# Two more seven-product units in the last down projection of an fp32 encoder layer, parked sums added a part earlier, parked data reloaded at other times

## The chip, the cores and the metric

The program runs on one core of a Trainium2 chip. The metric is the device time of one execution in microseconds (us); a time of three runs is their median.

## What is computed

One hybrid encoder layer on 256 tokens of width 2048, all in float32: a mixing sub-layer (neighbourhood attention beside a recurrent block), a SwiGLU feed-forward sub-layer, and a gated per-layer embedding, each with root-mean-square norms before and after. The change lies in the feed-forward sub-layer, cut from the reference to its core:

```python
fn = rms_norm(h, g_ffn_pre[i])                                              # (256, 2048)
ff = (jax.nn.silu(fn @ w_ffn_gate[i]) * (fn @ w_ffn_up[i])) @ w_ffn_down[i] # 2048 -> 5632 -> 2048
h = h + rms_norm(ff, g_ffn_post[i])
gate = jax.nn.sigmoid(rms_norm(h, g_ple_pre[i]) @ w_ple_gate[i])
h = h + rms_norm(gate * (p[i] @ w_ple_proj[i]), g_ple_post[i])
```

## The kernel before

**Matmuls.** Every float32 operand is split into a high part (rounded to the matmul's own float32 form) and a low part (the rest). A product of a 128x128 activation block and a 128x512 weight block is three matmuls on TensorE (PE): high times high, low times high, high times low. Weights come from HBM in tiles of two 128-row blocks by 512 columns (512 KB). SyncE (SP) issues the load into a raw buffer (`wr`, `third`, or a parked corner named `lower`, `lower2` or `ple`); ScalarE (ACT) casts it to `wh` (L624); VectorE (DVE) subtracts to get `wl` (L637); then the matmuls of that tile run. There are four `wh`/`wl` buffer pairs and, for part of the program, a fifth, `w`, which stands in the buffer that later holds the gain vector. A tile's raw buffer is free for the next load when DVE has subtracted it.

**Parts.** The 5632 hidden features are worked through in 11 groups of 512 columns (`f` = 0 to 10), in three parts: `PARTS = ((0, 4), (4, 8), (8, 11))`. In a part, each `f` has a gate and an up product with 2048 input features; ACT applies silu, DVE multiplies (`mid`, L1731) and transposes it in 32x32 blocks (L335), and 16 small DMAs (`mT<-mid`, L345) finish the transposition; ACT and DVE split the result to `mid0h/l`, `mid1h/l`, `mid2h/l`. Then the part's share of the down projection runs: four chunks of 512 output columns, taken in two pairs, `c` = 0 and 2. The third part has 12 feature blocks of 128, so each pair goes over six steps `k` = 0, 2, ..., 10.

**Parked sums.** The down products of parts 0 and 1 are copied out of PSUM by ACT (L1802) and written by SP (L1805) to two HBM tensors, `parts[0]` and `parts[1]`. In part 2 they return: `reload_sums` loads `parts[0]` into `mg` by SP (L1827) and adds `parts[1]` to it with accumulating DMAs issued by GpSimd (POOL, L593). The last chunks are then added to `mg` (L1472) and multiplied by the gain `g_ffn_post` (L1484). The residual stream `h` and a half of the embedding product `ple` are parked in HBM too, and their buffers lent out (`lower` stands in `h0`, `sums` in `h1`, `lower2` in `mg0`, `s` in `mg1`); `reload_h`, `reload_half` and `next_gain` bring back what is needed.

**Seven products.** A pair of chunks, the two row halves of the 256 tokens and the two blocks of a step `k` make eight block products. Some steps are done with seven (a 2x2 scheme in Strassen's manner), with sums of activations (`S1` to `S7`, made by DVE in `sums_of` and `mid_sums`) and sums of weights (DVE in `sum_stream`, one term by an accumulating DMA of POOL in `last_sum`). Such a unit runs as `four` (four products, two tiles), then, after DVE and ACT have put the four results together in the accumulators (`made_of_four`: ACT L730 and L724, DVE L732 to L739), `two` (two products) and a share of `one`. The `four`s are placed inside the group before, by `FOURS`; `TAKEN` says after which steps the `two`s and the `one`s come. Gate and up use it for `f` = 2 to 10, the down pairs for `k` in `DOWN_KS = {0: (0, 2), 2: (0, 2, 4)}`, in parts 0 and 1 only:

```python
SEVEN_PARTS = PARTS[:2]
...
mid, ks, DOWN_KS[c] if PARTS[part] in SEVEN_PARTS else (), apart=2 if end else 0,
```

**Order.** The PE's order is that of the segments. The other engines' order is made when the program is built: a planner (`Plan`) gives each operation an engine, a cost and a time from which it may start, and emits the one that can start first. On the chip each engine and each queue keeps that order, so an instruction that waits holds back all behind it on its engine.

Of the kernel before, what the change touches and what calls it, by code (L numbers as in the profile page):

```python
# [39 lines left out]
RING = 5  # L40
DOWN_KS = {0: (0, 2), 2: (0, 2, 4)}
SEVEN_F = range(2, 11)
SEVEN_PARTS = PARTS[:2]

SWAPPED = [
    (lambda f: (("w_ffn_gate", f), ("w_ffn_up", f)), SEVEN_F, SEVEN_KS),
    *(
        (lambda c: (("w_ffn_down", c), ("w_ffn_down", c + 1)), (c,), [4 * f0 + k for k in ks])
        for f0, _ in SEVEN_PARTS for c, ks in DOWN_KS.items()
    ),  # L50
]

# [183 lines left out]
def layer(ctx: ExitStack, tc: tile.TileContext, a: dict, out: bass.AP):  # L236
# [130 lines left out]
    def done(event):  # L367
        event.t = plan.now
# [63 lines left out]
    class Group:  # L432
# [39 lines left out]
        own, twos = None, None  # L472

        def issue(self, nxt):
            if self.own is None:
                self.own = []
            self.twos = []
            if nxt:
                nxt.own = []
            n, m = len(self.rest), len(self.rest) - self.apart  # L480
            begin = not self.sevens
# [12 lines left out]
            for i, k in enumerate(self.rest[:m]):  # L494
                for j, at in enumerate(FOURS[n, len(nxt.sevens)] if nxt and nxt.sevens else ()):
                    if i == at:
                        nxt.four(j)
                for ch, w, n0 in self.chunks:
                    seg(ch, w, n0, self.lhs, [k], begin and i == 0, i == n - 1,
                        self.after if i == m // 2 else None)  # L500
                take()
            for ch, w, n0 in self.chunks if self.apart else ():
                seg(ch, w, n0, self.lhs, self.rest[m:], first=False)

    TAKEN = {(3, 5): (0, 2, 3), (2, 6): (0, 1, 1, 1)}
    FOURS = {(8, 3): (3, 5, 7), (5, 3): (2, 3, 4), (6, 3): (3, 4, 5), (5, 2): (2, 4), (6, 2): (3, 5)}
    fours = {}

# [118 lines left out]
    def lo_stream():  # L627
        last_one = max(f[1] for f in fours.values())
        for i in range(len(tiles)):
            at_lo[0] = i  # L630
            for j in pieces(i):
                n = j.stop - j.start
                yield ev_hi[i, j.stop]
                src = raws[i] if n == 2 else raws[i][:, j, :]
                m = slice(j.start, j.start + src.shape[1])
                yield dve(src.shape[1] * N, give=gives.get(i) or raw_kind(i) if j.stop == 2 else None)
                nc.vector.tensor_tensor(  # L637
                    out=los[i][:, m, :], in0=src, in1=f32(his[i][:, m, :]), op=ALU.subtract
                )
                done(ev_lo[i, j.stop])  # L640
            raws.pop(i)
            if i == half_end:
                plan.add(reload_half(), plan.now + 76.0)
            if i in fours:
                plan.add(last_sum(i), plan.now, -2 * SOON)
            if i == last_one:
                done(ev_ple)

    MM = 0.216
    MM4 = 0.86  # L650
# [92 lines left out]
    def two_products(group, j, i):  # L743
        (C1, _, _), (C2, _, _) = group.chunks
        kx = group.sevens[j][1]
        s = group.lhs.sums[kx]
        plan.main(0, ev_lo[i, 2], group.lhs.ev[kx + 1], group.made)
        product(C1.accs[0], block(group.lhs, kx + 1, 0), i, 0, seeded=True)
        product(C2.accs[0], s["S4"], i, 1, seeded=True)
        spent(i)  # L750
        if i == last_two:
            for t in range(NT):
                plan.add(reload_sums(0, t), plan.clk["pe"] + 9.0 + 4.0 * t)
                plan.add(reload_sums(1, t), plan.clk["pe"] + 28.0 + 5.0 * t)
# [634 lines left out]
    t2 = {}  # L1389

    class Halves:
        def __init__(self, pool, n):
            self.tiles = [
                pool.tile([P, D], F32, tag=f"{n}{t}", name=f"{n}{t}") for t in range(NT)
            ]

# [204 lines left out]
            nc.sync.dma_start(spill[t], t2["h"].tiles[t])  # L1601
        done(ev_spilled)

    halves_back = []

    def reload_h(t):
        if "back" not in t2:
            t2["back"] = Halves(t2["pool"], "h")
        yield dma(1024)
        nc.sync.dma_start(t2["back"].tiles[t], spill[t])  # L1610
        halves_back.append(t)
        if len(halves_back) == NT:
            t2["h"] = t2["back"]
            done(ev_back)
# [128 lines left out]
    def carried(mid, kk0, mT):  # L1743
        summed = any(kk0 <= kx < kk0 + 4 for kx in mid.ev_sums)
        for b in range(0, 4, 2):
            kk = kk0 + b
            i, j = divmod(kk, 8)
            hi, lo = mid.tiles(i)
            yield from split(
                *(by_tile(x[:, j : j + 2, :]) for x in (hi, lo)), mT[:, b : b + 2], 2 * S,  # L1750
                give="mt" if b and not summed else None,
            )
            mid.pair(kk)
        if summed:
            plan.add(mid_sums(mid, kk0, mT), plan.now)

    def mid_sums(mid, kk0, mT):

# [35 lines left out]

    def down_post(part, c):
        def post(ch):
            e = None
            for t in range(NT):
                yield act(N, take=None if t else "mid")
                if not t:  # L1800
                    e = mid_tile()
                nc.scalar.copy(e[:, t, :], ch.accs[t])  # L1802
            ch.release()
            yield dma(512)
# [8 lines left out]
    ev_parts = []  # L1813

    def reload_sums(part, t):
        assert len(ev_parts) == 8
        if "mg_back" not in t2:
            t2["mg_back"] = t2["mg"] = Halves(t2["pool"], "mg")
        if part:
            there = Event()  # L1820
            yield from added(t2["mg"].tiles[t], parts[part][t], there)
            yield there
            if t == NT - 1:
                done(ev_sums_back)
        else:
            yield dma(1024)
            nc.sync.dma_start(t2["mg"].tiles[t], parts[0][t])  # L1827

    def after_ffn():
        return next_norm(ffn, hP, rstd_p, ev_rp, ("ple", "g_ple_post"))  # L1830
# [20 lines left out]
    for part, (f0, f1) in enumerate(PARTS):  # L1851
# [11 lines left out]
        for c in range(0, 4, 2):  # L1863
            slot = ring()
            end = last_part and c
            groups.append(Group(
                [
                    (Chunk(
                        sub_post(ffn, c + i, True, after_ffn) if last_part
                        else down_post(part, c + i), slot=slot,  # L1870
                    ), "w_ffn_down", (c + i) * N)
                    for i in range(2)
                ],
                mid, ks, DOWN_KS[c] if PARTS[part] in SEVEN_PARTS else (), apart=2 if end else 0,
                after=load_sqrt if end else None,
            ))
    n_ffn = len(segs)
# [176 lines left out]
    for i in range(min(fours), max(f[1] for f in fours.values())):  # L2054
        if i % (W_BUFS + MORE_W) < MORE_W:
            more_w[i] = i % (W_BUFS + MORE_W)
    for n, i in enumerate(sorted(lower)):
# [5 lines left out]
        gives[last] = tuple(f"t{j}" for j in js)  # L2063
    twos = [(j, i) for f, g, j, i in (s for s in segs if s[0] is two_products)]
    last_two = max(i for _, i in twos)
    half_end = max(f[1] for f in fours.values())
    i0 = segs[-1][-1]
    keep.update(range(i0, i0 + 8))
# [120 lines left out]
```

## Time and profile before

| | before |
|---|---|
| time of three runs, us | 1163.18 (1162.78 to 1164.9) |
| profiled execution, us | 1162.47 |
| its span from first to last instruction, us | 1160.7 |
| mean granted TensorE clock | 0.997 |
| PE busy, us | 1146.8 |
| DVE busy, us | 887.0 |
| ACT busy, us | 710.5 |
| POOL busy, us | 124.7 |

The span is cut by stage. Part 0's down products run from 509.5 us, part 1's from 759.1 us and part 2's from 982.1 us to about 1053 us; after them come the norm, the transposition of `h` and the gated embedding. Matmuls overlap, so their durations add up to more than the time between their starts: a stall is read from the starts.

### The profile page before, as it was taken

What the parts mean: (1) busy time and instruction counts of PE and PEld (TensorE: products, weight loads), DVE (VectorE), ACT (ScalarE), POOL (GpSimd) and SP (SyncE); (2) the same over time, 40 slices, a digit from 0 to 9 for tenths busy, and PEclk for the clock granted to TensorE, in tenths of its full rate; (3) what the DMA queues carried; (4) which work ended last, traced back from release to release, by engine and by line L of the source; (5) the groups of instructions that cost most, each with busy time, mean ns of one, the idle gap of its engine ahead of it and who ended that gap; (6) DMA issues with size and microseconds to landing.
All of it is one profiled execution on the core that took longest, in us unless ns stands there. A gap on an engine that the chain in (4) does not pass through costs nothing.

```text
span 1160.7 us, 15071 instructions
## 1 busy us (share of the span) xinstructions
PE 1146.8 (99%) x5219; PEld 951.5 (82%) x5219; DVE 887.0 (76%) x1107; ACT 710.5 (61%) x946; POOL 124.7 (11%) x202
## 2 busy tenths in 40 slices
PE   9999999999999999999999999999999999999997
PEld 8888888888888878888888888888888888777786
DVE  6678787888468878988778898988777985368565
ACT  6777777875556545655556566565565654256664
POOL 0000000000000023031000213312000321200000
PEclk9999999999999999999999999999999999999999
DMA  8867566545686987877876786778787677985771
GB/s 307 301 185 232 175 181 207 176 151 198 218 294 191 308 238 250 249 216 215 283 238 229 244 246 203 233 239 248 218 296 236 199 224 245 268 286 195 216 249 73
DMA packets 112732, 265.86 MB, mean 229 GB/s; under 512 B 39184, under 2 KB 46096, under 8 KB 110992
## 3 DMA queue, kind: packets, MB, share of 16 engines
q1 hardware_dynamic: 101744, 247.76, 63.2%
q0 software_dynamic: 10480, 16.79, 8.6%
q8 instruction: 41, 0.67, 0.2%
q10 hardware_dynamic: 432, 0.35, 0.1%
q14 instruction: 35, 0.29, 0.1%
HBM read 247.03 MB, written 9.44 MB: 221 GB/s over the span
## 4 chain that ended last, share of the span: by engine, by line
PE 88%; DMA 5%; DVE 3%; ACT 2%; issue 1%; POOL 1%; SPq 0%; ACTq 0%; DVEq 0%; POOLq 0%
PE acc L673 23%; PE acc L672 23%; PE acc L671 23%; PE acc L684 5%; PE acc L682 5%; PE acc L683 5%; DMA mT<-mid 2%; DMA wr<-in_w_ffn_down 1%; DMA wr<-in_w_ple_gate 1%; DVE wl L637 1%; ACT wh L624 1%; PE tr L326 1%; POOL mT L345 1%; PE warm L2098 0%; PE pg L357 0%
## 5 line engine op out<-in xcount | busy, mean ns | idle before, releaser
L637 DVE TENSOR_TENSOR wl<-wr,wh 128x1024 fp32r<-128x1024 f32 (+1 forms) x313 | 374.7, 1210 | 142.0 <-ACT wh L624 137.5
L624 ACT CAST wh<-wr 128x1024 fp32r<-128x1024 f32 (+1 forms) x313 | 324.7, 1043 | 213.0 <-PE acc L672 134.8
L672 PE MATMUL acc<-wh,hT_mix_lo 128*128 128x512 f32 x400 | 155.9, 390 | 0.3 <-DVE hT_mix_lo L315 0.3
L671 PE MATMUL acc<-wh,hT_mix_hi 128*128 128x512 f32 x400 | 156.0, 390 | 0.0
L673 PE MATMUL acc<-wl,hT_mix_hi 128*128 128x512 f32 x400 | 155.7, 389 | 0.0
L345 POOL DMA_DIRECT2D mT<-mid x152 | 89.0, 596 | 563.1 <-ACT wh L624 401.7
L673 PE MATMUL acc<-wl,hT_hi 128*128 128x512 f32 x320 | 124.6, 390 | 0.0
L671 PE MATMUL acc<-wh,hT_hi 128*128 128x512 f32 x316 | 124.5, 394 | 0.0
L672 PE MATMUL acc<-wh,hT_lo 128*128 128x512 f32 x316 | 123.2, 390 | 0.0
L624 ACT CAST wh<-ple 128x1024 fp32r<-128x1024 f32 (+1 forms) x54 | 53.4, 989 | 68.0 <-DVE ple L576 34.4
L672 PEld LDWEIGHTS acc<-wh,hT_mix_lo 128*128 128x128 f32 x400 | 75.1, 188 | 16.4 <-DVE hT_mix_lo L315 1.0
L671 PEld LDWEIGHTS acc<-wh,hT_mix_hi 128*128 128x128 f32 x400 | 75.1, 188 | 15.5
L673 PEld LDWEIGHTS acc<-wl,hT_mix_hi 128*128 128x128 f32 x400 | 75.1, 188 | 15.5
L637 DVE TENSOR_TENSOR wl<-ple,wh 128x1024 fp32r<-128x1024 f32 (+1 forms) x54 | 61.5, 1142 | 12.7 <-ACT wh L624 12.2
L673 PEld LDWEIGHTS acc<-wl,hT_hi 128*128 128x128 f32 x320 | 60.3, 188 | 12.9
L672 PEld LDWEIGHTS acc<-wh,hT_lo 128*128 128x128 f32 x316 | 59.4, 188 | 11.5
L671 PEld LDWEIGHTS acc<-wh,hT_hi 128*128 128x128 f32 x316 | 59.5, 188 | 11.4
L593 POOL DMA_DIRECT2D ple<-in_w_ffn_up x27 | 24.0, 891 | 234.7 <-DVE wl L637 195.9
L671 PE MATMUL acc<-wh,hT_ffn_hi 128*128 128x512 f32 x104 | 40.9, 393 | 0.8 <-ACT hT_ffn_hi L313 0.8
L672 PE MATMUL acc<-wh,hT_ffn_lo 128*128 128x512 f32 x104 | 40.8, 393 | 0.5 <-DVE hT_ffn_lo L315 0.5
L673 PE MATMUL acc<-wl,hT_ffn_hi 128*128 128x512 f32 x104 | 40.5, 390 | 0.0
L671 PE MATMUL acc<-wh,mid2h 128*128 128x512 f32 x96 | 38.3, 399 | 2.2 <-ACT wh L624 2.2
(431 smaller groups left out, 2422.6 us busy)
## 6 DMA issues: line engine op xcount, KB each, us to landing
wr<-in_w_ffn_gate SPq DMA_DIRECT2D x78, 512.0 KB, 5.4
wr<-in_w_in SPq DMA_DIRECT2D x77, 512.0 KB, 4.6
wr<-in_w_ffn_down SPq DMA_DIRECT2D x65, 512.0 KB, 5.5
wr<-in_w_ffn_up SPq DMA_DIRECT2D x49, 512.0 KB, 5.1
wr<-in_w_out SPq DMA_DIRECT2D x32, 512.0 KB, 4.4
wr<-in_w_ple_gate SPq DMA_DIRECT2D x32, 512.0 KB, 4.6
lower<-in_w_ffn_up SPq DMA_DIRECT2D x22, 512.0 KB, 6.0
ple<-in_w_ffn_up POOLq DMA_DIRECT2D x27, 256.0 KB, 4.3
```

What stands on the lines that cost most here:

```text
L326: nc.tensor.transpose(tr[:, b, t * P : (t + 1) * P], e[:, t, sl], ident)
L345: (nc.gpsimd if i in pool else nc.sync).dma_start(dst[32 * j : 32 * j + 32, :, :, i, :], src[32 * i : 32 * i + 32, :, :, j, :],)
L593: nc.gpsimd.dma_start(dst, src, accum_op=ALU.add)
L624: nc.scalar.copy(his[i][:, 0 : src.shape[1], :] if n == 2 else his[i][:, j, :], src)
L637: nc.vector.tensor_tensor(out=los[i][:, m, :], in0=src, in1=f32(his[i][:, m, :]), op=ALU.subtract)
L671: nc.tensor.matmul(accs[t], hi[:, sl], his[i][:, j, :], start=st, stop=False, **group)
L672: nc.tensor.matmul(accs[t], lo[:, sl], his[i][:, j, :], start=False, stop=False, **group)
L673: nc.tensor.matmul(accs[t], hi[:, sl], los[i][:, j, :], start=False, stop=sp, **group)
L682: nc.tensor.matmul(dst, x[0], wh, start=start, stop=False, skip_group_check=seeded)
L683: nc.tensor.matmul(dst, x[1], wh, start=False, stop=False, skip_group_check=seeded)
L684: nc.tensor.matmul(dst, x[0], wl, start=False, stop=stop, skip_group_check=seeded)
```

## The change

- **Seven products in the last part.** Pair `c` = 0 of part 2 does steps `k` = 0 and 2 as units of seven products (the weights' host layout follows). Its `four`s stand in the gate and up group of `f` = 10. The sums of its activations are made 20 us later on the planner's clock than the split they come from.
- **The last features used later.** The first step of the next pair (`c` = 2, `k` = 0) is put inside pair `c` = 0, after its step `k` = 6 (`pair`, `ahead`), so that steps 8 and 10, which use the last group's features, stand behind it.
- **Parked sums added early.** Part 1's down chunks are no longer copied by ACT. POOL loads the slice of `parts[0]`, DVE adds the accumulators to it, and POOL writes the sum to `parts[1]`. The accumulating DMAs of `reload_sums` are gone. Part 0's slices are written by POOL instead of SP.
- **Parked data back at other times.** `mg` is loaded once, from `parts[1]`, after the last `one` of gate and up; `h0` and `h1` after the last `two`; the gain right after the last use of `w`; the half of `ple` 46 instead of 76 on the planner's clock after the last `four`.

The diff, cut to what the prediction speaks of:

```diff
-        for f0, _ in SEVEN_PARTS for c, ks in DOWN_KS.items()
+        for f0, _ in PARTS for c, ks in DOWN_KS.items() if not c or f0 != PARTS[-1][0]
...
+        def pair(self, i):
+            n = len(self.rest)
+            for ch, w, n0 in self.chunks:
+                seg(ch, w, n0, self.lhs, [self.rest[i]], not self.sevens and i == 0, i == n - 1,
+                    self.after if i == (n - self.apart) // 2 else None)
...
-                for ch, w, n0 in self.chunks:
-                    seg(ch, w, n0, self.lhs, [k], begin and i == 0, i == n - 1,
-                        self.after if i == m // 2 else None)
+                if i >= self.ahead:
+                    self.pair(i)
+                if nxt and nxt.apart and i == 1:
+                    nxt.pair(0)
+                    nxt.ahead = 1
...
-    TAKEN = {(3, 5): (0, 2, 3), (2, 6): (0, 1, 1, 1)}
+    TAKEN = {(3, 5): (0, 2, 3), (2, 6): (0, 1, 1, 1), (2, 4): (0, 2, 1)}
...
         if i == last_two:
-            for t in range(NT):
-                plan.add(reload_sums(0, t), plan.clk["pe"] + 9.0 + 4.0 * t)
-                plan.add(reload_sums(1, t), plan.clk["pe"] + 28.0 + 5.0 * t)
-                plan.add(reload_h(t), plan.clk["pe"] + 50.0 + 12.0 * t)
+            plan.add(reload("h", 0), plan.clk["pe"] + 3.0)
+            plan.add(reload("h", 1), plan.clk["pe"] + 15.0)
+        if i == mg1_end:
+            plan.add(reload("mg", 0), plan.clk["pe"] + 6.0)
+            plan.add(reload("mg", 1), plan.clk["pe"] + 14.0)
...
         if i == max(more_w):
-            plan.add(next_gain(("ffn", "g_ffn_post"), plan.clk["pe"] + 37.0), plan.clk["pe"] + 37.0)
+            plan.add(next_gain(("ffn", "g_ffn_post"), plan.clk["pe"]), plan.clk["pe"])
...
     def down_post(part, c):
         def post(ch):
+            if part:
+                yield ("pool", COST["move"], None, "mid", None)
+                e, here = mid_tile(), Event()
+                nc.gpsimd.dma_start(e, parts[0].rearrange("t p d -> p t d")[:, :, sl])
...
             for t in range(NT):
+                if part:
+                    yield dve(N)
+                    nc.vector.tensor_tensor(
+                        out=e[:, t, :], in0=ch.accs[t], in1=e[:, t, :], op=ALU.add
+                    )
...
-            nc.sync.dma_start(
-                parts[part].rearrange("t p d -> p t d")[:, :, c * N : (c + 1) * N], e
-            )
+            nc.gpsimd.dma_start(parts[part].rearrange("t p d -> p t d")[:, :, sl], e)
```

**How the order moves.** In the rows below an operation is written as out<-in with its shape; equal neighbours stand as one row with a count, and buffer numbers are mostly left out. SP's queue around the end of part 2's gate and up and its down products, before:

```order
L532 DMA wr<-in_w_ffn_down 128x1024 x3
L1827 DMA mg_8134<-part_98 128x2048
L532 DMA wr<-in_w_ffn_down 128x1024 x2
L1827 DMA mg_8135<-part_98 128x2048
L532 DMA wr<-in_w_ffn_down 128x1024 x2
L345 DMA mT<-mid 32x8x32 x8
L532 DMA wr<-in_w_ffn_down 128x1024 x4
L1424 DMA gain_g_ffn_post<-in_g_ffn_post 128x2048
L532 DMA wr<-in_w_ffn_down 128x1024 x7
L1610 DMA h_8136<-h_spill 128x2048
```

And now, from the gain on:

```order
L1431 DMA gain_g_ffn_post<-in_g_ffn_post 128x2048
L538 DMA wr<-in_w_ffn_down 128x1024
L538 DMA lower<-in_w_ffn_down 128x1024
L538 DMA wr<-in_w_ffn_gate 128x1024
L538 DMA wr<-in_w_ffn_up 128x1024
L538 DMA wr<-in_w_ffn_down 128x1024
L538 DMA third<-in_w_ffn_down 128x1024
L1826 DMA mg_8229<-part_101 128x2048
L1826 DMA mg_8259<-part_101 128x2048
L538 DMA wr<-in_w_ffn_down 128x1024 x4
L344 DMA mT<-mid 32x8x32 x8
L538 DMA wr<-in_w_ffn_down 128x1024 x4
```

The gain, which stood behind the last features' `mT`, now stands ahead of the two tiles of the second `four` (the first `wr` and `lower`); both `mg` loads stand together, and ahead of `mT`. POOL's queue from the middle of part 1's down products to its last DMA, before:

```order
L593 DMA ple<-in_w_ffn_down 128x512 x3
L593 DMA ple<-in_w_ffn_up 128x512 x6
L345 DMA mT<-mid 32x8x32 x16
L593 DMA ple<-in_w_ffn_up 128x512 x3
L345 DMA mT<-mid 32x8x32 x24
L593 DMA mg_8134<-part_101 128x2048
L593 DMA mg_8135<-part_101 128x2048
```

And now, from the stores of part 1's first down pair on (`part_98` is `parts[0]`, `part_101` is `parts[1]`, `ple` takes the accumulated weight terms):

```order
L1813 DMA part_101<-mid 128x2x512 x2
L599 DMA ple<-in_w_ffn_up 128x512 x3
L1796 DMA mid<-part_98 128x2x512 x2
L1813 DMA part_101<-mid 128x2x512 x2
L599 DMA ple<-in_w_ffn_up 128x512 x3
L344 DMA mT<-mid 32x8x32 x16
L599 DMA ple<-in_w_ffn_up 128x512 x3
L344 DMA mT<-mid 32x8x32 x14
L599 DMA ple<-in_w_ffn_down 128x512
L344 DMA mT<-mid 32x8x32 x2
L599 DMA ple<-in_w_ffn_down 128x512
L344 DMA mT<-mid 32x8x32 x8
```

The two accumulating loads of `mg` are gone from its end; loads and stores of slices and two accumulated weight terms have come in between the moves. DVE's order around the end of the last gate and up group (`f` = 10), before:

```order
L637 TENSOR_TENSOR wl<-wr,wh 128x1024
L309 TENSOR_TENSOR mid2l_7784<-mT,mid2h_7783 128x512
L637 TENSOR_TENSOR wl<-wr,wh 128x1024 x5
L1731 SCALAR_TENSOR_TENSOR mid<-acc_7828,rstd_f,mid 128x512
L1731 SCALAR_TENSOR_TENSOR mid<-acc_7829,rstd_f,mid 128x512
L335 STREAM_TRANSPOSE mid<-mid 128x1024
L637 TENSOR_TENSOR wl<-wr,wh 128x1024 x4
L309 TENSOR_TENSOR mid2l_8349<-mT,mid2h_8348 128x512 x2
```

And now:

```order
L643 TENSOR_TENSOR wl<-wr,wh 128x1024 x3
L738 TENSOR_TENSOR u<-u,acc_8165 128x512
L740 TENSOR_TENSOR u<-u,acc_8163 128x512
L743 TENSOR_TENSOR acc_8165<-acc_8164,u 128x512
L745 TENSOR_TENSOR acc_8164<-acc_8164,u 128x512
L643 TENSOR_TENSOR wl<-wr,wh 128x1024
L643 TENSOR_TENSOR wl<-third,wh 128x1024
L1726 SCALAR_TENSOR_TENSOR mid<-acc_7829,rstd_f,mid 128x512
L1726 SCALAR_TENSOR_TENSOR mid<-acc_7830,rstd_f,mid 128x512
L334 STREAM_TRANSPOSE mid<-mid 128x1024
L643 TENSOR_TENSOR wl<-lower,wh 128x1024 x2
L643 TENSOR_TENSOR wl<-wr,wh 128x1024 x4
```

Four additions of `made_of_four` now stand between the subtractions of the tiles for the end of gate and up and those for the first down step (`k` = 4).

More of the change, by code (lines that the diff above doesn't have):

```diff
@@ L470, in one @@
             segs.append((one_product, self, js, i))
-        own, twos = None, None
+        own, twos, ahead = None, None, 0
+        def pair(self, i):
[3 more added lines that the diff above has]
+                    self.after if i == (n - self.apart) // 2 else None)
         def issue(self, nxt):
@@ L480, in issue @@
             n, m = len(self.rest), len(self.rest) - self.apart
-            begin = not self.sevens
             more = []
@@ L641, in lo_stream @@
             raws.pop(i)
+            if i == last_one:
+                done(ev_ple)
             if i == half_end:
-                plan.add(reload_half(), plan.now + 76.0)
+                plan.add(reload_half(), plan.now + 46.0)
             if i in fours:
                 plan.add(last_sum(i), plan.now, -2 * SOON)
-            if i == last_one:
-                done(ev_ple)
     MM = 0.216
@@ L1391, in layer, with __init__ @@
     class Halves:
-        def __init__(self, pool, n):
-            self.tiles = [
+        def __init__(self, pool, n, tiles=None):
+            self.tiles = tiles or [
                 pool.tile([P, D], F32, tag=f"{n}{t}", name=f"{n}{t}") for t in range(NT)
@@ L1602, in spill_h @@
         done(ev_spilled)
[L1604 to L1614, printed above, removed]
     half_spill = ctx.enter_context(
@@ L1754, in carried @@
         if summed:
-            plan.add(mid_sums(mid, kk0, mT), plan.now)
+            plan.add(mid_sums(mid, kk0, mT), plan.now + (20.0 if mid.name[-1] == str(2) else 0.0))
     def mid_sums(mid, kk0, mT):
@@ L1796, in post @@
         def post(ch):
-            e = None
-            for t in range(NT):
[L1799 to L1802, printed above, removed]
+            sl = slice(c * N, (c + 1) * N)
+            if part:
+                yield ("pool", COST["move"], None, "mid", None)
+                e, here = mid_tile(), Event()
+                nc.gpsimd.dma_start(e, parts[0].rearrange("t p d -> p t d")[:, :, sl])
+                plan.now += COST["landing"]
+                done(here)
+                yield here
+            for t in range(NT):
+                if part:
[3 more added lines that the diff above has]
+                    )
+                else:
+                    yield act(N, take=None if t else "mid")
+                    if not t:
+                        e = mid_tile()
+                    nc.scalar.copy(e[:, t, :], ch.accs[t])
             ch.release()
-            yield dma(512)
-            nc.sync.dma_start(
-                parts[part].rearrange("t p d -> p t d")[:, :, c * N : (c + 1) * N], e
-            )
+            yield ("pool", COST["move"], None, None, None)
+            nc.gpsimd.dma_start(parts[part].rearrange("t p d -> p t d")[:, :, sl], e)
             plan.now += COST["landing"]
@@ L1811, in down_post, with reload @@
         return post
[L1813 to L1827, printed above, removed]
+    ev_parts, back = [], {}
+    def reload(n, t):
+        assert n == "h" or len(ev_parts) == 8
+        yield dma(1024)
+        if (n, t) not in back:
+            back[n, t] = t2["pool"].tile([P, D], F32, tag=f"{n}{t}", name=f"{n}{t}")
+        nc.sync.dma_start(back[n, t], (spill if n == "h" else parts[1])[t])
+        if len([k for k in back if k[0] == n]) == NT:
+            t2[n] = Halves(None, n, [back[n, k] for k in range(NT)])
+            done(ev_back if n == "h" else ev_sums_back)
     def after_ffn():
@@ L1873, in layer @@
                 ],
-                mid, ks, DOWN_KS[c] if PARTS[part] in SEVEN_PARTS else (), apart=2 if end else 0,
+                mid, ks, () if end else DOWN_KS[c], apart=2 if end else 0,
                 after=load_sqrt if end else None,
@@ L2053, in layer @@
                 more_raws[i] = n % (R_BUFS + MORE_RAWS)
-    for i in range(min(fours), max(f[1] for f in fours.values())):
+    for i in range(min(fours), max(f[1] for f in fours.values() if f[4] is hF.ev_sums)):
         if i % (W_BUFS + MORE_W) < MORE_W:
@@ L2065, in layer @@
     last_two = max(i for _, i in twos)
+    mg1_end = max(f[5] for f in fours.values() if f[4] is hF.ev_sums)
     half_end = max(f[1] for f in fours.values())
```

1 line of the change is left out of this document (removed).

## The prediction

> **What bounds the kernel now.** I read the page first, then the waits of PE, then PE's own timeline around the longest of them, and last ACT and the DMA of that stretch.
>
> ```profile
> span 1160.7 us, 15071 instructions
> PE 1146.8 (99%) x5219; PEld 951.5 (82%) x5219; DVE 887.0 (76%) x1107; ACT 710.5 (61%) x946; POOL 124.7 (11%) x202
> ```
>
> ```profile
> PE acc L671 <- ACT wh L624: 2.2, 2, 1.2
> PE acc L673 <- DVE wl L637: 1.0, 2, 0.5
> PE acc L671 <- ACT hT_ffn_hi L313: 0.8, 1, 0.8
> PE acc L672 <- DVE hT_ffn_lo L315: 0.5, 1, 0.5
> ```
>
> PE is the bound: a matmul saved is time saved, unless PE waits. Of its waits in the feed-forward stage the first two rows, 3.2 us, are the ones in reach of the change. They lie here (PE's timeline: start, duration, what; in brackets the idle time and its releaser):
>
> ```profile
> 1003.19 0.39 PE L671 MATMUL acc<-wh,mid2h 128*128 128x512 f32 x1
> ...
> 1009.08 0.39 PE L673 MATMUL acc<-wl,mid2h 128*128 128x512 f32 x1
> 1010.51 0.50 PE L671 MATMUL acc<-wh,mid2h 128*128 128x512 f32 x1 [1.05 <-ACT wh L624]
> ...
> 1011.77 0.50 PE L673 MATMUL acc<-wl,mid2h 128*128 128x512 f32 x1 [0.52 <-DVE wl L637]
> ...
> 1013.95 0.39 PE L673 MATMUL acc<-wl,mid2h 128*128 128x512 f32 x1
> 1015.50 0.50 PE L671 MATMUL acc<-wh,mid2h 128*128 128x512 f32 x1 [1.16 <-ACT wh L624]
> ...
> 1021.44 0.39 PE L671 MATMUL acc<-wh,mid2h 128*128 128x512 f32 x1
> ```
>
> From 1003.19 to 1009.08 lie 26 steps, so a matmul takes 0.2265 us from start to start. From 1009.08 to 1021.44, 12.36 us, lie 28 steps, worth 6.34 us: 6.0 us are lost here, nearly twice the idle time that the waits show. The rest is the clock (time, busy per engine, then clock, DMA share, GB/s):
>
> ```profile
> 1017.60:1021.00 3.40, 3.40 (x10) 2.66 (x9) 3.20 (x5) 2.55 (x5) 0.00 (x0) 0.50 0.82 231
> ```
>
> 3.4 us at half clock cost 1.7 us. Why PE waited, ACT's timeline says, and the DMA issues (count, KB, median us to landing) in 955 to 975 us (one row) and 985 to 1000 us (four rows):
>
> ```profile
> 1003.14 1.05 ACT L624 CAST wh<-wr 128x1024 fp32r<-128x1024 f32 x1 [5.35 <-DMA wr<-in_w_ffn_down]
> 1009.42 1.04 ACT L624 CAST wh<-wr 128x1024 fp32r<-128x1024 f32 x1 [5.23 <-DMA wr<-in_w_ffn_down]
> ```
>
> ```profile
> wr<-in_w_ffn_down SPq DMA_DIRECT2D x4, 512.0 KB, 5.6
> ```
>
> ```profile
> wr<-in_w_ffn_down SPq DMA_DIRECT2D x6, 512.0 KB, 14.0
> mg<-part POOLq DMA_DIRECT2D x2, 1024.0 KB, 14.8
> gain_g_ffn_post<-in_g_ffn_post SPq DMA_DIRECT2D x1, 1024.0 KB, 20.1
> mT<-mid POOLq DMA_DIRECT2D x8, 32.0 KB, 2.4
> ```
>
> Two accumulating loads of `mg` and the gain stood in the DMA together, and the weight tiles issued around them landed after 14.0 us instead of 5.6.
>
> **The change, part by part.**
>
> *Matmuls.* Each unit does 21 matmuls where the eight products took 24; two units save 6 x 0.2265 = 1.36 us. All stands on PE's path.
>
> *The stall.* The accumulating loads are gone, and `parts[0]` with them from this stage: of four passes of 1 MB over `mg` two remain. The gain moves to the end of the last `w` tile; the `mg` loads go ahead of `mT`. What is left between 990 and 1020 us is one load of `h`, behind eight weight tiles. I take the whole 6.0 us as saved; what if not is a rival below. I count the half clock with it, since it follows the second gap at once and no other place of the stage shows one. [...]
>
> *DVE.* The group rows, all shapes apart (count, busy us, mean ns):
>
> ```profile
> L637 DVE TENSOR_TENSOR wl<-wr,wh 128x1024 fp32r<-128x1024 f32 x307 | 370.7, 1220 | 140.9 <-ACT wh L624 136.4 <-PE acc L672 1.2 <-DMA sq<-ev 0.3
> L576 DVE TENSOR_TENSOR ple<-ple,lower 128x512 f32<-128x512 f32 x30 | 20.7, 691 | 3.6 <-DMA lower<-in_w_ffn_up 1.7 <-DMA lower<-in_w_ffn_down 1.0
> L737 DVE TENSOR_TENSOR acc<-acc,u 128x512 f32<-128x512 f32 x13 | 9.1, 699 | 0.4
> L1766 DVE TENSOR_TENSOR mT<-mT 128x256 f32<-128x256 f32 x8 | 3.4, 422 | 0.2
> L309 DVE TENSOR_TENSOR sums<-mT,sums 128x1024 fp32r<-128x1024 f32 x2 | 2.4, 1219 | 0.0
> L730 ACT COPY u<-acc 128x512 f32<-128x512 f32 x13 | 7.5, 578 | 3.6 <-PE acc L684 3.6
> ```
>
> New in part 2: six weight sums (6 x 0.69), four additions in the accumulators (4 x 0.70), the activation sums (4 x 0.42 + 1.22) and three more subtractions (7 tiles instead of 4; 3 x 1.22): 13.5 us, nearly all between 955 and 995 us (columns PE, PEld, DVE, ACT, POOL):
>
> ```profile
> 955.00:995.00 40.00, 40.00 (x178) 33.13 (x177) 22.84 (x22) 19.01 (x23) 12.72 (x21) 1.00 0.75 228
> 900.00:940.00 40.00, 40.00 (x178) 33.11 (x178) 35.96 (x39) 23.43 (x27) 12.02 (x19) 1.00 0.74 225
> ```
>
> 22.84 + 13.5 = 36.3 of 40 us. The second row shows DVE at 35.96 with PE never short; this hides it. If that cover is gone, PE loses what DVE runs over.
>
> The tightest place is behind the second `four`: its four results must be joined before the first `k` = 4 tile, and that tile's subtraction now stands behind the additions: 0.58 (L730) + 4 x 0.70 + 1.22 = 4.6 us, while one step of gate and up, 24 x 0.2265 = 5.4 us, runs on PE. 0.8 us is left for four hand-overs. I take 0.4 us lost; bounds 0 and 1.2 (one subtraction).
>
> *Moves.* The `mT` buffer is single, and that of `f` = 8 is now held until its sums are made; behind the transposition of `f` = 9 (four additions and three subtractions, 4 x 0.42 + 3 x 1.22 = 5.3 us); so the moves of `f` = 9 start that much later, and two of them stand behind a weight term on POOL. POOL's, PE's and DVE's rows:
>
> ```profile
> 952.57 8.73 POOL L345 DMA_DIRECT2D mT<-mid  x15 [0.55 <-issue]
> ```
>
> ```profile
> 962.16 0.39 PE L673 MATMUL acc<-w,hT_mix_hi 128*128 128x512 f32 x1
> ...
> 981.88 0.39 PE L673 MATMUL acc<-wl,hT_mix_hi 128*128 128x512 f32 x1
> ```
>
> ```profile
> 994.52 1.30 DVE L309 TENSOR_TENSOR mid2l<-mT,mid2h 128x512 fp32r<-128x512 f32 x2 [1.97 <-DMA wr<-in_w_ffn_down]
> ```
>
> The moves of `f` = 9 end near 968 and land after 2.4 us; ACT's casts of them stand ahead of the second `four`'s, which PE reaches at 979.4 (962.4, the end of the last `w` tile, plus 75 matmuls), with some 6 us of DVE and ACT between. About 3 us are spare: I take 0, bounds 0 and 2. The last features' first step comes 90 matmuls, 20.4 us, after the end of gate and up, before 96, 21.7 us; they were ready 14 us after it (994.52 + 1.30 against the last gate and up matmul at 981.88), so this costs nothing. SP's eight `mT` now wait for the transposition with four weight tiles issued ahead of them, 48 matmuls or 10.9 us of PE work.
>
> *Part 1's down chunks.* ACT loses eight copies, DVE gains eight additions (about 0.70 each, 2.8 us per pair). They wait for POOL's load of a slice:
>
> ```profile
> 811.67 0.87 POOL L593 DMA_DIRECT2D ple<-in_w_ffn_down  x1 [7.79 <-DVE wl L637]
> ```
>
> ```profile
> 821.15 1.27 ACT L1802 COPY mid<-acc 128x512 f32<-128x512 f32 x2
> ```
>
> POOL is free at 812.5 and the chunk is full at 821.1: the load has 8.6 us, beside 5.6 for an equal weight tile. Behind the additions wait only subtractions with a lead. Zero; with the 14.0 of the disturbed tiles they would hold DVE 5.4 us, less than the four buffered tiles (10.9 us) by which it may be ahead.
>
> *After the down products* nothing moves but the half of `ple`, now just ahead of the gain for the last stage, a transfer that PE does not wait for. The two waits on `hT_ffn` (1.3 us) I leave; a quieter queue could take them away, so they are the low bound.
>
> **The sum.** 1162.47 - 1.36 - 6.0 + 0.4 = 1155.5 for an execution like the profiled one, which lies 0.7 under the median: 1156.2. In the likeliest case 1154.5 (the 0.4 and the 1.3 gone) to 1159.0 (both upper bounds).
>
> **The rivals.**
>
> *The stall only moves.* The tiles of the last pair come late behind `h`, or DVE falls behind once more, with the same gap and half clock. For it: the weight stream is as dense. Against it: nothing accumulates there. Only the matmuls are saved: 1161.8.
>
> *The gain holds up the second `four`* (slower). It now stands in SP's queue ahead of that unit's two tiles. Landings of the three gain loads (us, min/median/max):
>
> ```profile
> DMA to landing us min/median/max: 6.0/8.1/20.1
> ```
>
> It is issued when PE leaves the last `w` tile, at 962.4. The two tiles must be there by about 974.5 (979.4 less two sums, cast, subtraction and hand-overs). With 6.0 or 8.1 us it is out by 970.5; with 20.1 it lands at 982.5 and the tiles about 2 us later: 10 us of stall, with a half clock 11.7, gives 1167.5. It decides from a landing later than about 10 us on. Against it: the 20.1 was measured beside both accumulating loads.
>
> [...]
>
> *The change does not save its matmuls*: PE's order has six rows fewer, so this is out.
>
> **How the numbers follow.** Likeliest case 0.73, the stall moves 0.12, the gain 0.09, the half clock stays 0.06. About 0.2% (2.3 us) is what a measurement of this kernel can tell from no change: faster is below 1160.9, slower above 1165.5. The likeliest and the half clock are faster, and a fifth of the moved stall: 0.81; the rest of that is the same, 0.10; the gain is slower, 0.09. The range from 1154.5 to 1161.5 leaves out the gain and part of the moved stall.
>
> **What the changed profile would show.** Right: no wait of PE for a cast or a subtraction near 1010 us, clock 1.00 there, the last down product's end some 7 us earlier, weight tiles landing in 4 to 6 us, DVE near 90% from 955 to 995. Wrong: a PE gap at about 980 us with the gain's landing over 10 us; gaps at 988 behind DVE's additions; at 821 or 866 DVE waiting for a DMA of `mid`; a gap from 1000 to 1040.

## The result, and the profile after

The changed kernel takes 1159.46 us (median of eight executions, 1158.84 to 1162.11) against 1164.99 (median of eight, 1162.78 to 1168.89): the ratio is 0.9957, 95% interval 0.9943 to 0.997, so it is faster by some 5.0 us (5.5 between the medians) where 7.0 were forecast. Its profiled execution took 1159.04 us, 3.4 less than that of before. Page and waits of PE of the changed kernel:

```profile
span 1157.1 us, 15105 instructions
PE 1144.7 (99%) x5213; PEld 949.7 (82%) x5213; DVE 903.7 (78%) x1133; ACT 711.1 (61%) x944; POOL 133.5 (12%) x214
```

```profile
PE acc L688 <- ACT wh L630: 2.2, 1, 2.2
...
PE acc L690 <- DVE wl L643: 1.3, 2, 0.8
...
PE acc L678 <- DVE hT_ffn_lo L314: 0.5, 1, 0.5
```

PE has six matmuls fewer, and the waits of the `mid2h` products (3.2 us before) are gone. The stretch of the old stall, the issues of 985 to 1000 us and the landing of the gain (min/median/max), all of the changed kernel:

```profile
1000.00:1020.00 20.00, 20.00 (x90) 16.57 (x89) 12.03 (x12) 9.58 (x11) 0.53 (x1) 1.00 0.89 300
```

```profile
wr<-in_w_ffn_down SPq DMA_DIRECT2D x4, 512.0 KB, 4.9
```

```profile
DMA to landing us min/median/max: 5.7/5.7/5.7
```

PE is busy throughout at full clock, and the weight tiles land after 4.9 us instead of 14.0. But there are two new losses. PE's timeline at both, and the engines that it waited for:

```profile
425.70 0.39 PE L679 MATMUL acc<-wl,hT_mix_hi 128*128 128x512 f32 x1
428.28 0.50 PE L688 MATMUL acc<-wh,sf 128*128 128x512 f32 x1 [2.19 <-ACT wh L630]
...
429.80 0.50 PE L690 MATMUL acc<-wl,sf 128*128 128x512 f32 x1 [0.79 <-DVE wl L643]
...
984.06 0.50 PE L690 MATMUL acc<-wl,sums 128*128 128x512 f32 x1 [0.53 <-DVE wl L643]
```

```profile
424.40 1.14 ACT L306 CAST mid0h<-mT 128x512 fp32r<-128x512 f32 x2 [9.10 <-DMA mT<-mid]
427.18 1.04 ACT L630 CAST wh<-ple 128x1024 fp32r<-128x1024 f32 x1 [1.64 <-DVE ple L582]
...
978.62 1.15 ACT L306 CAST mid2h<-mT 128x512 fp32r<-128x512 f32 x2 [5.78 <-DMA mT<-mid]
981.69 1.05 ACT L630 CAST wh<-ple 128x1024 fp32r<-128x1024 f32 x1 [1.92 <-DVE ple L582]
```

```profile
979.28 0.69 DVE L308 TENSOR_TENSOR mid2l<-mT,mid2h 128x512 fp32r<-128x512 f32 x1 [5.12 <-ACT mid2h L306]
979.89 0.69 DVE L578 TENSOR_TENSOR ple<-wr 128x512 f32<-128x512 f32 x1
```

Both have one shape. ACT stands idle 9.1 and 5.8 us for the moves of a group's features (`mT<-mid`), and DVE 8.1 and 5.1 us behind it, although nothing needs those features yet; the weight sums of the next `four` are queued behind the split, and PE runs out of tiles. At 426 us a half clock follows:

```profile
430.00:432.00 2.00, 2.00 (x6) 1.27 (x5) 1.93 (x4) 2.00 (x3) 0.93 (x1) 0.57 0.17 20
432.00:434.00 2.00, 2.00 (x6) 1.48 (x6) 2.00 (x3) 2.00 (x3) 0.00 (x0) 0.58 0.89 150
```

A loss is counted here, as in the prediction, from the starts of the matmuls: all time between two starts beyond 0.2265 us. That gives 5.2 us at 425.7 to 433.2 (before 1.2) and 1.4 us at 982.5 to 985.8 (before none). Profile to profile: -1.36 (matmuls), -5.96 (the stall), +1.38 (at 982), +4.03 (at 426), -0.99 (the wait for `hT_ffn` at 1093) come to -2.9 us, where the spans differ by -3.6; the rest lies ahead of 350 us, 0.6 us of it less at one transposition.

The loss at 426 is the puzzle: no instruction has moved on any engine up to there.

### The profile page after: what moved, and what is told of

Its sections match the earlier page's. It is cut to its first block, busy times and chain, and to the rows that moved or that the text cites. A ratio compares the mean times of both kernels' runs of the same rounds, so it can differ in the third digit from the quotient of the medians.

```text
span 1157.1 us, 15105 instructions
## 1 busy us (share of the span) xinstructions
PE 1144.7 (99%) x5213; PEld 949.7 (82%) x5213; DVE 903.7 (78%) x1133; ACT 711.1 (61%) x944; POOL 133.5 (12%) x214
## 4 chain that ended last, share of the span: by engine, by line
PE 93%; DMA 3%; DVE 1%; ACT 1%; POOL 1%; issue 1%; ACTq 0%; DVEq 0%
PE acc L678 24%; PE acc L679 24%; PE acc L677 24%; PE acc L690 5%; PE acc L689 5%; PE acc L688 5%; DMA mT<-mid 3%; PE tr L325 1%; POOL mT L344 1%; DMA wr<-in_w_ffn_gate 1%; DVE wl L643 0%; PE pg L356 0%; PE pg L357 0%; PE pg L355 0%; DVE h L1548 0%
## 5 line engine op out<-in xcount | busy, mean ns | idle before, releaser
L643 DVE TENSOR_TENSOR wl<-wr,wh 128x1024 fp32r<-128x1024 f32 (+1 forms) x309 | 369.7, 1210 | 117.0 <-ACT wh L630 113.5
L630 ACT CAST wh<-wr 128x1024 fp32r<-128x1024 f32 (+1 forms) x309 | 320.3, 1043 | 197.0 <-PE acc L678 142.7
L630 ACT CAST wh<-ple 128x1024 fp32r<-128x1024 f32 (+1 forms) x57 | 56.4, 992 | 76.4 <-DVE ple L582 42.9
L643 DVE TENSOR_TENSOR wl<-ple,wh 128x1024 fp32r<-128x1024 f32 (+1 forms) x57 | 65.3, 1147 | 13.0 <-ACT wh L630 12.5
L643 DVE TENSOR_TENSOR wl<-third,wh 128x1024 fp32r<-128x1024 f32 x31 | 37.8, 1219 | 5.5 <-ACT wh L630 5.5
L630 ACT CAST wh<-third 128x1024 fp32r<-128x1024 f32 x31 | 32.6, 1051 | 14.8 <-PE acc L678 10.0
```

The lines of the kernel that those rows point to most:

```text
L630: nc.scalar.copy(his[i][:, 0 : src.shape[1], :] if n == 2 else his[i][:, j, :], src)
L643: nc.vector.tensor_tensor(out=los[i][:, m, :], in0=src, in1=f32(his[i][:, m, :]), op=ALU.subtract)
```

## The experiments

Comparisons are with executions of the kernel before on the same chip; its median there was 1165.67 (experiments 1 to 4), 1164.71 (5 to 7) and 1166.33 us (10). These are three chips, so a difference between medians of two of these groups is less sure than one within a group; the ratios are given beside it.

**1. The split of f = 0 queued later, in the changed kernel.**

```diff
-            plan.add(carried(mid, kk0, mT), plan.now + (0.5 if soon else 3.0), -SOON if soon else 0.0)
+            plan.add(carried(mid, kk0, mT), plan.now + (0.5 if soon else 14.0 if f == 0 else 3.0), -SOON if soon else 0.0)
```

> The changed kernel with one planner delay longer: the split of f = 0's features to mid0 (ACT cast, DVE subtraction) is queued about 11 us later, behind the two `four` tiles that follow, so that a late landing of `mT<-mid` no longer holds ACT and DVE. In the changed kernel's profile PE loses 5.2 us at 425.7 to 433.2 us there. Theory A (that loss is the landing of f = 0's moves, it varies from execution to execution and is in the kernel before as well, where the profile shows 1.2 us of it): the loss falls under 0.5 us and the time to about 1154.5 (1159.5 less 5), with a narrower spread. Theory B (the loss is a cost of the change, from its own queues): the split stands elsewhere, but what made the moves late remains and something else waits for them; the time stays at 1158 to 1160.

1154.97 us (1153.38 to 1155.81); ratio to before 0.9907 (0.9891 to 0.9922). Nothing is lost near 426 us any more, and the time fell by 4.5 us between the medians (5.8 by the two ratios): theory A.

**2. The same edit in the kernel before.**

> The kernel before with the same single edit. Theory A: the kernel before loses 1 to 5 us at the same place in its timed executions (its profile, 1162.47, was the lowest of eight), so its median falls by 2 to 4 us, to about 1161 to 1163, and its spread narrows. Theory B: only the 1.2 us of its profile can be won, a median near 1163.8.

1159.73 us (1158.66 to 1160.1); ratio 0.9949 (0.9932 to 0.9966). This is 5.9 us less, more than theory A asked for and five times the 1.2 us of the old profile. So the executions that are timed seem to lose about 6 us at f = 0 (experiment 8 looks at one more). The stall of the last part is still there: 5.2 us of loss, `wr` landing after 14.1.

**3. Only the parked sums added early, in the kernel before.**

```diff
                 plan.add(reload_sums(0, t), plan.clk["pe"] + 9.0 + 4.0 * t)
-                plan.add(reload_sums(1, t), plan.clk["pe"] + 28.0 + 5.0 * t)
...
-            yield from added(t2["mg"].tiles[t], parts[part][t], there)
...
-            nc.sync.dma_start(t2["mg"].tiles[t], parts[0][t])
+        nc.sync.dma_start(t2["mg"].tiles[t], parts[1][t])
```

(with `down_post` as in the change)

> The kernel before with only the parked sums changed: part 1's down chunks are added to part 0's by DVE and written by POOL, and `mg` is loaded once; no unit of seven products is added, gain and `h` come back at the old times. My prediction's step: the two accumulating loads made the stall at 1009 to 1021 us, so nearly all of the 6.0 us is saved, the profile has no wait there, and the weight tiles land in 5 to 7 us; about 1159 (1165 less 6), and the changed kernel's remaining advantage is its 1.4 us of matmuls less its own 1.4 us loss at 982 us. Rival (the stall came from the gain and the bytes in all): 1 to 3 us saved, a gap remains behind the gain.

1161.2 us (1158.69 to 1161.89); ratio 0.9957 (0.994 to 0.9974). The last down products show no wait, even with the gain at its old place; issues of 985 to 1000 us:

```profile
wr<-in_w_ffn_down SPq DMA_DIRECT2D x5, 512.0 KB, 5.1
gain_g_ffn_post<-in_g_ffn_post SPq DMA_DIRECT2D x1, 1024.0 KB, 8.0
```

So this part of the change takes the whole stall away, as predicted. The medians show 4.5 us of it (5.0 by the ratio). The two profiled executions show only 1.0, because this one lost 6.1 us at f = 0, with 6.8 us of half clock, where the old profile had lost 1.2.

**4. Only the gain moved, in the kernel before.**

```diff
-            plan.add(next_gain(("ffn", "g_ffn_post"), plan.clk["pe"] + 37.0), plan.clk["pe"] + 37.0)
+            plan.add(next_gain(("ffn", "g_ffn_post"), plan.clk["pe"]), plan.clk["pe"])
```

> The kernel before with only the gain moved: it is loaded when PE has left the last `w` tile, ahead of part 2's down tiles, and not beside the accumulating loads, which stay. Theory (the accumulating loads alone make the weight tiles late): the stall stays at 4 to 6 us, the time within 1.5 us of the kernel before. Rival (three MB at once, of which the gain is the third): the tiles land by about 9 us instead of 14 and the stall falls to under 2 us, a gain of about 4 us.

1163.39 us (1160.71 to 1164.33); ratio 0.9979 (0.997 to 0.9989). Neither side was right: the weight tiles still landed late, but in the profile the loss there fell from 6.0 to 2.6 us, with gaps of 1.15 and 0.53 us and no half clock, and the median by 2.3 us.

```profile
wr<-in_w_ffn_down SPq DMA_DIRECT2D x6, 512.0 KB, 12.7
mg<-part POOLq DMA_DIRECT2D x2, 1024.0 KB, 14.9
```

**5. Both splits out of the way.** Experiment 1, and the activation sums of part 2 planned earlier, which frees `mT` for the moves of f = 9:

```diff
-            plan.add(mid_sums(mid, kk0, mT), plan.now + (20.0 if mid.name[-1] == str(2) else 0.0))
+            plan.add(mid_sums(mid, kk0, mT), plan.now + (10.0 if mid.name[-1] == str(2) else 0.0))
```

> The changed kernel with the late split of f = 0 and, beside it, the sums of part 2's first activations planned 10 instead of 20 us after their split, so that `mT` is free and the moves of f = 9 start some 8 us earlier. The changed kernel and the late-split one both lose 1.4 us at the second `four` (982 and 977 us). Theory (those 1.4 us are the moves of f = 9 landing late, with the split queued ahead of that unit's weight sums): the gap goes, 1.2 to 1.4 us less than the late-split kernel, about 1153.6. Rival (DVE is too full around the second `four`, by additions and subtractions): the gap stays or shifts, no gain, 1155.

1152.84 us (1152.65 to 1155.59); ratio 0.99 (0.9882 to 0.9919): 2.1 us below experiment 1 between the medians, of two chips, but only 0.8 us by the ratios, whose intervals overlap. It is the lowest median here. POOL's first move of f = 9, ACT's first cast of it, and all waits of PE in this profile:

```profile
951.54 2.97 POOL L344 DMA_DIRECT2D mT<-mid  x5 [15.07 <-ACT w L630]
```

```profile
966.12 0.62 ACT L306 CAST mid2h<-mT 128x512 fp32r<-128x512 f32 x1 [1.53 <-DMA mT<-mid]
```

```profile
PE final L2034 <- ACT diag L2032: 2.0, 1, 2.0
PE warm L2101 <- POOL ones L290: 1.1, 1, 1.1
PE acc L678 <- DVE hT_ffn_lo L314: 0.5, 1, 0.5
PE acc L678 <- DVE hT_mix_lo L314: 0.3, 1, 0.3
```

Against experiment 1, which like this one loses nothing at f = 0, the moves start 4.1 us earlier (955.66 there; some 8 were expected) and the cast comes 7.0 us earlier (973.16 there). PE has no gap at the second `four`, with the same work on DVE: the rival is out.

**6. The change without its units.** Experiment 1, with no units of seven in part 2 and `h` back at the times of before:

```diff
-                mid, ks, () if end else DOWN_KS[c], apart=2 if end else 0,
+                mid, ks, () if last_part else DOWN_KS[c], apart=2 if end else 0,
...
-            plan.add(reload("h", 0), plan.clk["pe"] + 3.0)
-            plan.add(reload("h", 1), plan.clk["pe"] + 15.0)
+            plan.add(reload("h", 0), plan.clk["pe"] + 50.0)
+            plan.add(reload("h", 1), plan.clk["pe"] + 62.0)
```

> The changed kernel with the late split of f = 0, but without its two units of seven products in part 2 (`h` back at the times of the kernel before). It has six matmuls more, 1.36 us, and no second `four` that could wait at 977 us (1.35 us in the late-split kernel's profile). Theory (the units win their matmuls and lose the same to the late moves of f = 9): equal to the late-split kernel within 0.5 us, 1155. Rival (the 1.35 us would be lost in another place anyway): 1.4 us slower, 1156.4.

1156.09 us (1154.73 to 1160.26), between the two. The profiled execution was the slowest of the six; it lost 4.5 us at 1089 us, where PE waits for `hT_ffn`, and 1.9 us in the first 11 us of the program. Inconclusive, hence experiment 10.

**7. The same bytes, not accumulated.** In the kernel before:

```diff
-            yield from added(t2["mg"].tiles[t], parts[part][t], there)
+            yield ("pool", COST["move"] , None, None, None)
+            nc.gpsimd.dma_start(t2["mg"].tiles[t], parts[part][t])
+            plan.now += ADDED
+            done(there)
```

> The kernel before with the two accumulating loads of `mg` made plain loads of the same bytes at the same place (part 0's sums are left out of the result). Theory (it is the accumulating that is slow and that slows the weight tiles): the 1 MB loads land in 6 to 10 us instead of 14.8, the weight tiles in 6 to 9 instead of 14.0, and the stall at 1009 to 1021 us falls from 6.0 to under 1.5 us; the time falls by 4 to 6 us, to about 1160. Rival (the bytes in flight are what counts): landings of 12 us and more, the stall stays over 4 us, the time within 1.5 us of the kernel before.

1158.98 us (1158.08 to 1162.73); ratio 0.9951 (0.9936 to 0.9966). The order on each engine is that of before, and the stall is gone altogether. Issues of 985 to 1000 us, and PE over the old stall:

```profile
wr<-in_w_ffn_down SPq DMA_DIRECT2D x6, 512.0 KB, 8.2
mg<-part POOLq DMA_DIRECT2D x2, 1024.0 KB, 9.5
gain_g_ffn_post<-in_g_ffn_post SPq DMA_DIRECT2D x1, 1024.0 KB, 13.1
```

```profile
1000.00:1025.00 25.00, 25.00 (x112) 20.71 (x111) 15.26 (x18) 13.92 (x20) 0.00 (x0) 1.00 0.93 364
```

It is the accumulating that made the stall, not the bytes that were loaded; by experiment 4 the gain beside it made it longer.

**8 and 9. Before and after once more, for a second profile each.**

> The kernel before once more, for a second profile of the same program. Theory A (the loss at f = 0's moves varies between executions of one program, and its first profile, 1162.47 us with 1.2 us lost at 427 to 430, was a quick one beside a median of 1165): 3 to 6 us are lost there now, and the time is about 1165 to 1167. Theory B (the program fixes it): 1.2 us again.

> The changed kernel once more. Theory A: 1 to 6 us lost at 425 to 433, other than the 5.2 us of its first profile, and the time moves by as much; the 1.4 us at 982, which come from the order of the moves of f = 9, stay within 0.5 us. Theory B: 5.2 us again.

Before took 1165.06 us and lost 5.9 us at f = 0, with the same program that had lost 1.2 (one execution each, here and below); PE's row there, and the clock after it:

```profile
427.58 0.80 PE L682 MATMUL acc<-wh,sf 128*128 128x512 f32 x1 [2.19 <-ACT wh L624]
```

```profile
428.00:434.00 6.00, 5.70 (x14) 3.88 (x14) 5.93 (x8) 5.52 (x6) 0.95 (x1) 0.50 0.42 77
```

After took 1158.55 us, with 4.2 us lost at f = 0 and 1.9 at the second `four`. Theory A both times.

**10. The kernel before with the early sums and the late split.**

> The kernel before with the parked sums added early and with the late split of f = 0, so that neither the accumulating loads nor the first loss blur the comparison. Against the late-split kernel before (1159.73) it shows what the stall at 1009 to 1021 was worth: theory, 4.3 to 5.3 us (the losses of that kernel's profile there), so 1154.4 to 1155.4. Against the late-split changed kernel (1154.97) it shows what the two units bring net: theory, nothing within 0.5 us (1.36 us of matmuls less 1.35 at the second `four`). Rival (the early additions and the slice loads cost something as well): 1156 or more.

The edits of experiments 2 and 3 together: 1155.15 us (1153.39 to 1155.77); ratio 0.9901 (0.9884 to 0.9918). Against experiment 2 the early sums win 4.6 us (5.6 by the ratios, whose intervals lie apart); against experiment 1 the units win 0.2 us, or lose 0.7 by the ratios, nothing that these spreads could tell from zero.

The losses of PE (us) in the profiles, with the profiled execution's time:

| kernel | time | at 426 | second `four` | at 1007-1030 | `hT_ffn`, 1085-1100 |
|---|---|---|---|---|---|
| before | 1162.47 | 1.2 | - | 6.0 | 1.3 |
| before again (8) | 1165.06 | 5.9 | - | 5.4 | 1.0 |
| before, late split (2) | 1159.07 | 0 | - | 5.2 | 0.6 |
| before, gain early (4) | 1160.71 | 2.3 | - | 2.6 | 2.2 |
| before, sums early (3) | 1161.44 | 6.1 | - | 0 | 1.5 |
| before, plain loads (7) | 1162.73 | 6.0 | - | 0 | 1.8 |
| sums early, late split (10) | 1155.19 | 0 | - | 0 | 1.5 |
| after | 1159.04 | 5.2 | 1.4 | 0 | 0.3 |
| after again (9) | 1158.55 | 4.2 | 1.9 | 0 | 0.9 |
| after, late split (1) | 1155.36 | 0 | 1.4 | 0 | 2.1 |
| after, late split, no units (6) | 1160.26 | 0 | - | 0 | 4.5 |
| after, both (5) | 1152.98 | 0 | 0 | 0 | 0.6 |

Less its four losses an execution with the units comes to 1151.6 to 1152.4, one without them to 1152.7 to 1154.0 (experiments 7 and 6, in which the program's start took 1.7 and 1.9 us longer than in before, 1154.9 and 1155.7): about the 1.36 us of six matmuls apart. So the table holds nearly all that differs.

## Why the prediction was right, and where not

*Matmuls: right.* Six fewer, and the sums above lie apart by about their 1.36 us. Yet as the change stands the units earn nothing (experiment 10), since they brought the wait at the second `four`; with that wait removed the profiled execution of experiment 5 lies 2.2 us below that of experiment 10, 1.36 of it matmuls and 0.9 a shorter wait for `hT_ffn`. That the units pay is not shown by the times: the medians lie 2.3 us apart, but on two chips, and the ratios are 0.99 and 0.9901.

*The stall: right in place, cause and size.* Experiments 3 and 7 show the cause, 2 and 10 its price, 4.6 us between medians and 5.2 to 6.0 in the profiles of before. That the gain would matter too was in the text ("stood in the DMA together"); experiment 4 gives it a share: taken away alone it leaves 2.6 us in the one profile. The stall did not move elsewhere; that rival is out.

*The half clock: gone with the gaps*, as taken. Where PE had no gap the clock was 1.00: from 1000 to 1020 us in after and in experiment 3, and to 1025 in experiments 7 and 10. A half clock that stays there without a gap, to which the prediction gave 0.06, is shown by no run. But a gap did not always bring one. In before, 3.4 us at 0.50 followed gaps of 1.05, 0.52, 1.16 and 0.52 us; its second profile has gaps of 1.12, 0.53, 1.23 and 0.53 us at the same place, and clock 1.00 from 1010 to 1024; experiment 4 has 1.15 and 0.53 us, and its matmuls go on about 0.23 us apart behind them. At f = 0, 3.4 us at half clock followed gaps of 2.19 and 0.79 us in after, and 6.8 us came with gaps of 2.19 and 0.30 us in the second profile of before. So the half clock of before did follow the stall, as the prediction had it, but a stall of this size need not bring one: that differs between executions, and what decides it was not shown.

*DVE: hidden, as taken.* The stretch from 955 to 995 is fuller, but less than the 36.3 us worked out:

```profile
955.00:995.00 40.00, 39.40 (x172) 31.69 (x172) 32.12 (x37) 21.78 (x25) 11.25 (x18) 1.00 0.79 263
```

It has 32.1 of 40 us, with 5.1 us idle for the late moves, and some of the new work lies outside. Behind the additions at 988 us no matmul waits: the 0.4 us set down for the tightest place were not lost there.

*Moves of f = 9: the step that failed.* "About 3 us are spare: I take 0." It cost 1.4 and 1.9 us, inside its bounds of 0 and 2. POOL's row of the first move in before (the row in the prediction has the 15 others), and its rows in the changed kernel:

```profile
951.38 0.64 POOL L345 DMA_DIRECT2D mT<-mid  x1 [14.44 <-DVE mid L335]
```

```profile
961.12 2.97 POOL L344 DMA_DIRECT2D mT<-mid  x5 [19.73 <-DVE sums L308]
964.27 5.25 POOL L344 DMA_DIRECT2D mT<-mid  x9 [0.19 <-issue]
969.51 0.97 POOL L599 DMA_DIRECT2D ple<-in_w_ffn_down  x1
970.11 0.99 POOL L344 DMA_DIRECT2D mT<-mid  x1
972.35 0.59 POOL L344 DMA_DIRECT2D mT<-mid  x1 [1.24 <-DMA mT<-mid]
```

In this stretch PE of the changed kernel runs 3.3 us behind PE of before, which comes from the start and from 426 us, so 3.3 us come off before times are compared. The moves then start 6.4 us later than before, not 5.3, and the last of them ends at 969.6 instead of near 968: 1.6 us. From that end (972.9 as measured) to the cast at 978.6 there were 5.7 us instead of the 2.4 of the landing row used: 3.3 us, the larger part. Together they are 4.9 us, and 3 were spare. The landing was taken from a stretch of before, and so was the traffic around it. The same 18 us, from about the first move on, in before and in after (last two columns: DMA share and GB/s):

```profile
952.00:970.00 18.00, 18.00 (x81) 14.92 (x80) 11.80 (x13) 9.52 (x11) 8.68 (x16) 1.00 0.51 128
```

```profile
961.00:979.00 18.00, 18.00 (x81) 14.92 (x80) 12.80 (x13) 6.62 (x8) 10.32 (x17) 1.00 0.84 255
```

The moves now run beside twice the bytes: the gain, issued at 965.9, and six weight tiles from 969.4 on. The gain seems to have a part in this: the move issued at 965.4, just ahead of it, landed after 2.5 us, and the next one, at 966.0, after 6.1, half a microsecond behind the gain. It is not the part that the rival gave it: it landed in 5.7 us, and the unit's weight tiles were in time. The moves were not. How much of the delay is the gain's was not tried; in experiment 5 all moves but the last go ahead of it, and the sixteen land after a median of 4.1 us all the same (4.5 in after; 2.3 for fourteen of them in before), so it is not the gain alone.

*Part 1's down chunks: right.* DVE's eight additions never waited:

```profile
L1803 DVE TENSOR_TENSOR mid<-acc,mid 128x512 f32<-128x512 f32 x8 | 5.1, 683 | 0.0
```

*After the down products.* The waits for `hT_ffn` went from 1.3 to 0.3 us and then to 0.9; over all profiles they lie between 0.3 and 4.5. They vary by execution; that a quieter queue takes them away, as the low bound had it, is not shown.

*The base of the sum: failed, and covered by the range by chance.* The prediction set the profiled execution 0.7 us under the median of three. Over all executions of before it is a quick one, 2 to 4 us under the medians, as it lost 1.2 us at 427 where four profiles of kernels with the same order up to there lost 5.2 to 6.1 (two more 2.3 and 4.2). Part of it was among PE's waits, but not among the rows shown, and was passed over as out of the change's reach:

```profile
PE acc L684 <- DVE wl L637: 0.7, 1, 0.7
```

It is out of its reach, but it moves the time by as much as the change does: the profile of after had 4.0 us more of it. The last down product starts at 1050.53 instead of 1053.17, 2.6 us earlier and not 7; without those 4.0 us it would be 6.7.

```profile
1053.17 0.39 PE L673 MATMUL acc<-wl,mid2h 128*128 128x512 f32 x1
```

```profile
1050.53 0.39 PE L679 MATMUL acc<-wl,mid2h 128*128 128x512 f32 x1
```

So the time lies 3.3 us above the forecast of 1156.2: some 1.8 us by the base (1164.99 against 1163.18), and about 1.4 by the second `four`. That it is still inside the range is luck: the range's upper end was set for a stall that moves in part, and not for a base that is off.

## What to carry to other kernels

An operation that waits for a DMA holds all that is queued behind it on its engine (in after, near 424 us, 9.1 us on ACT and 8.1 on DVE): queue it by when its result is needed and by the slowest landing that the profiles show, not by the first time it could run. Before a sum is made against one profile, see in a second profile of the same program which losses stay; here the largest one differed by 4.7 us between two executions. A transfer's price belongs to its neighbours: take its landing from the stretch where it will run, and count what an accumulating load does to the plain loads beside it (here a median landing of 14.0 us, and of 8.2 beside plain loads of the same bytes).

## What the runs showed of the hardware

An accumulating 1 MB load took 14.8 to 15.1 us to land (median of two, in four profiles) and a plain one of the same bytes, at the same place and from the same queue, 9.5 (experiment 7). The 512 KB tiles issued beside them, from 985 to 1000 us, landed after a median of 12.7 to 14.1 and of 8.2 us. The latest took 17.1 us in before. The second profile of before, which runs 3.2 us later there (gain issued at 996.2 instead of 993.0), has a median of 5.7 for the five tiles of that window, and PE still waited 1.12 and 1.23 us for casts. Sixteen small moves under a full DMA (f = 0; share 0.98 from 400 to 424 us in before) had a median landing of 6.1 us in one execution of before and 7.4 in another, and the cast behind them came at 421.8 and 423.7 us. PE was 1.5 us ahead in the second, so by its matmuls the cast was 3.4 us later. That cost 4.7 us, most of it through the clock: 2.5 us of idle time in the second execution (2.19 and 0.30) came with 6.8 us at half clock, which cost another 3.4 us.
